# A two-layer diffusion trunk whose instruction order is planned with other durations

## The chip, the cores and the metric

The kernel runs on one NeuronCore of a Trainium2 chip. The metric is the device time of one execution in microseconds (us). Three runs of the kernel before gave 1421.18, 1422.88 and 1425.69 us; the median is 1422.88 us.

## The reference, cut to what matters

The reference is a trunk of two layers over 256 latent tokens and 256 context tokens, each of width 1024. Each layer does this:

```
mod          = silu(c) @ w_ada + b_ada                      # shifts, scales and gates, 6 x 1024
a            = rms_norm(h) * (1 + scale) + shift
p            = a @ w_in                                     # one input projection for three mixers
fa           = real 2-D Fourier transform of p's first 512 columns
db           = differential attention, 4 heads, two softmaxes each, with rotary embedding
nc           = neighbourhood attention, 8 heads, with a position bias
y            = (sig(g_a)*(fa@w_a) + sig(g_b)*(db@w_b) + sig(g_c)*(nc@w_c)) @ w_out
h            = h + gate * y
f            = rms_norm(h) * (1 + scale2) + shift2
h            = h + gate2 * (silu(conv(f@w_up_a)) * conv(f@w_up_b)) @ w_down     # 2 x 2816 wide
```

Layer 0 computes latent and context tokens (512 tokens), layer 1 only the latent ones for all that comes after keys and values (256 tokens). The result is the final RMS norm of the latent stream. Everything is float32.

## The kernel before

**Products.** Each float32 product is made of three passes over rounded values: every operand is split into a high part (rounded to the format that TensorE reads quickly, `F32R`) and a low part (the rest). `three()` (L246, matmuls on L250) and `tok_part()` (L267, matmuls on L276) multiply high by high, high by low and low by high into one PSUM bank. A matmul of layer 0 has 512 columns, one of layer 1 has 256.

**Weights.** `unit()` (L103) brings 512 KB of weights (128 x 1024) in by one DMA from SyncE (L100) into one of four raw buffers `wr`; ScalarE (ACT) makes the high part by a cast (L110), VectorE (DVE) the low part by a subtraction (L111). There are three pairs of split buffers, `wa`, `wb` and `wc`, used in turn. One unit feeds 24 matmuls of `feat()` (8 blocks of the inner dimension, three passes each).

**Stages.** The stretches of the trace, in us from the span's start, are these:

- 0 to 36: inputs, first modulation vectors, first norms; 36 to 107: values and keys in token layout (`tok_part`).
- 107 to 285: attention of layer 0. There are eight items, four heads of differential attention (`diff_head`, L351) and four pairs of neighbourhood heads (`na_pair`, L401), in turn. `project()` (L624) makes queries and keys of the next item by two `feat_tile`s and is written ahead of the item itself.
- 285 to 462: the three branch projections, gates and merge (L681 to L707).
- 462 to 570: output projection, residual, second norm. 570 to 853: the feed-forward (conv, silu, `w_down`).
- 853 to 960: layer 1's norm and token-layout products. 960 to 1138: attention of layer 1 with the Fourier mixer at its end. Layer 1 also computes the pre-activations of one of the gates there (L646, L647) and keeps them in `h`.
- 1138 to 1245: merge, output projection and norm of layer 1. 1245 to 1406: feed-forward. 1406 to the end: final norm and output.

**Attention on the engines.** A tile of scores is made in one of three PSUM banks `sc` (two matmuls, L337 and L339). In `na_pair` DVE adds the bias (L432) and takes the maximum (L434), ACT takes the exponential (L437), DVE scales (L408, L409), TensorE transposes (L414), ACT copies the transpose to SBUF (L415), TensorE multiplies by the values (L421). The bank of the scores is free again after the exponential. In `diff_head` the same steps are L364, L366, L369 to L372, L306, L308 and L377. The accumulators of the projections are two banks `pp`; a `pp` bank is free when queries or keys have been copied out (`rope`, `stack_k`, `stack_q`, L317 to L349).

**Sigmoids.** The merge takes the sigmoid of a gate into a tile `p` of a pool with three buffers. In layer 1 that pool is open during the attention. The sigmoid of the one gate whose pre-activations lie in `h` is L694, the others are on L697 (straight from the accumulator).

**What sets the order.** The Python code writes all instructions once, in one sequence. The framework's scheduler then plays the program through in a model of time, and in it hands each engine, whenever that engine is free, the earliest written of those of its instructions whose inputs and buffers are ready. The result is one fixed list for each engine (TensorE, VectorE, ScalarE, GpSimd, and SyncE for the DMAs), and on the chip every engine works its list strictly in order, waiting where an input isn't there. So the durations in the model decide which matmul of the next item stands between which two steps of this one. In the lists of before, long stretches of TensorE's keep the written order (merge and feed-forward of both layers); the matmuls of L250 in the attention stages are cut into short groups, with scores, transposes and value products of the item before in between.

## Time and profile before

| | |
|---|---|
| median of three runs | 1422.88 us |
| the profiled execution | 1424.49 us |
| its span, first to last instruction | 1422.7 us |
| TensorE busy | 1378.5 us, 97% |
| VectorE busy | 938.0 us, 66% |
| ScalarE busy | 686.7 us, 48% |
| GpSimd busy | 144.0 us, 10% |
| mean granted TensorE clock | 0.99 |
| DMA | 206 MB, 145 GB/s over the span |

The busy time of an engine is the union of its instructions' records; what is missing to the span is time in which the engine ran nothing. The granted clock is the share of TensorE's full 2.4 GHz that was granted; 0.5 is its lower level, 1.2 GHz. "L250 PE MATMUL pp<-aH,wch" is a matmul of line 250 with output tile `pp` and the inputs `aH` and `wch`. `PE` is TensorE, `PEld` its weight loads, `DVE` VectorE, `ACT` ScalarE, `POOL` GpSimd. "A <- B" in a list of waits says that A's engine had nothing to do until B ended.

### The profile page before, as it was taken

The page shows a single profiled execution, that of the slowest core. Times are in us where ns is not written, and L with a number is a line of the kernel's source. Part 1 is how long each engine was busy: PE and PEld are TensorE (multiplying, and loading weights), DVE is VectorE, ACT ScalarE, POOL GpSimd, SP SyncE. Part 2 cuts the span into 40 slices and gives each one's busy share as a digit, 9 for nine tenths or more (in the row PEclk, how much of TensorE's full clock was granted, in tenths as well). Part 3 has the DMA queues.
Part 4 walks back from the last instruction along what each step waited for, and adds up shares of the span by engine and source line. Part 5 has one row for each costly group of instructions (what it writes and reads, how often), then busy time and mean ns, then how long its engine had stood idle before and what let it go on. Part 6 is the DMA issues. An engine that isn't in the chain of part 4 may idle for free. (4 is left out here: it accounts for less than half of the span.)

```text
span 1422.7 us, 21634 instructions
## 1 busy us (share of the span) xinstructions
PE 1378.5 (97%) x8470; PEld 1206.7 (85%) x8470; DVE 938.0 (66%) x1552; ACT 686.7 (48%) x1188; POOL 144.0 (10%) x136
## 2 busy tenths in 40 slices
PE   6999999999999999999999999999998999999998
PEld 4887778888888798888888888998787899899997
DVE  3447876487877747878877573527677456788843
ACT  4547776532222335443433222527666545666643
POOL 1100000011211230000000021201000012200001
PEclk9999999999999999999999999999999999999999
DMA  7732211256556322444645682423333355466663
GB/s 274 260 107 75 74 57 48 75 165 219 180 190 197 129 75 89 149 148 134 206 136 168 200 264 91 152 89 111 97 90 104 95 188 177 146 190 187 185 177 97
DMA packets 60390, 206.14 MB, mean 145 GB/s; under 512 B 6656, under 2 KB 9088, under 8 KB 60288
## 3 DMA queue, kind: packets, MB, share of 16 engines
q1 hardware_dynamic: 60288, 204.76, 45.4%
q8 instruction: 66, 1.08, 0.3%
q14 instruction: 36, 0.29, 0.1%
HBM read 203.69 MB, written 1.05 MB: 144 GB/s over the span
## 5 line engine op out<-in xcount | busy, mean ns | idle before, releaser
L111 DVE TENSOR_TENSOR wcl<-wr,wch 128x1024 fp32r<-128x1024 f32 x93 | 114.8, 1234 | 92.4 <-ACT wch L110 92.4
L110 ACT CAST wch<-wr 128x1024 fp32r<-128x1024 f32 x93 | 97.7, 1051 | 145.2 <-PE pp L250 51.8
L110 ACT CAST wbh<-wr 128x1024 fp32r<-128x1024 f32 (+1 forms) x93 | 96.0, 1032 | 137.0 <-PE pp L250 47.5
L110 ACT CAST wah<-wr 128x1024 fp32r<-128x1024 f32 (+1 forms) x94 | 97.0, 1032 | 129.4 <-PE pp L250 33.0
L111 DVE TENSOR_TENSOR wbl<-wr,wbh 128x1024 fp32r<-128x1024 f32 (+1 forms) x93 | 111.5, 1199 | 69.6 <-ACT wbh L110 69.6
L111 DVE TENSOR_TENSOR wal<-wr,wah 128x1024 fp32r<-128x1024 f32 (+1 forms) x94 | 112.8, 1200 | 47.7 <-ACT wah L110 47.1
L250 PE MATMUL pp<-aH,wch 128*128 128x256 f32 (+1 forms) x272 | 90.9, 334 | 1.2 <-ACT aH L231 1.2
L250 PE MATMUL pp<-aH,wcl 128*128 128x256 f32 (+1 forms) x272 | 90.7, 333 | 0.0
L250 PE MATMUL pp<-aL,wch 128*128 128x256 f32 (+1 forms) x272 | 90.3, 332 | 0.0
L158 DVE SCALAR_TENSOR_TENSOR wr<-wr,cr 128x1024 f32<-128x1024 f32 x44 | 55.4, 1258 | 40.4 <-DMA wr<-in_wadaT 40.2
L250 PE MATMUL pp<-aL,wbh 128*128 128x512 f32 (+1 forms) x216 | 77.6, 359 | 1.4 <-DVE aL L707 1.4
L250 PE MATMUL pp<-aH,wbh 128*128 128x512 f32 (+1 forms) x216 | 78.1, 362 | 0.0
L250 PE MATMUL pp<-aH,wbl 128*128 128x512 f32 (+1 forms) x216 | 77.8, 360 | 0.0
L703 POOL TENSOR_TENSOR m<-m,o 128x512 f32<-128x512 f32 (+1 forms) x32 | 46.2, 1444 | 288.4 <-DVE o L702 288.4
L187 POOL TENSOR_TENSOR sqa<-sqa,t 128x256 f32<-128x256 f32 x18 | 21.2, 1193 | 492.6 <-DMA wr<-in_wdn 264.1
L250 PE MATMUL pp<-aH,wah 128*128 128x256 f32 (+1 forms) x200 | 66.4, 332 | 1.5 <-DVE ks L332 1.5
L250 PE MATMUL pp<-aH,wal 128*128 128x256 f32 (+1 forms) x200 | 66.0, 330 | 0.0
L250 PE MATMUL pp<-aL,wah 128*128 128x256 f32 (+1 forms) x200 | 65.8, 329 | 0.0
L250 PE MATMUL sc<-aL,wah 128*128 128x512 f32 (+1 forms) x192 | 64.6, 336 | 0.4 <-DVE aL L707 0.4
L250 PE MATMUL sc<-aH,wah 128*128 128x512 f32 (+1 forms) x192 | 64.6, 336 | 0.0
L250 PE MATMUL sc<-aH,wal 128*128 128x512 f32 (+1 forms) x192 | 64.3, 335 | 0.0
L250 PE MATMUL sc<-aH,wch 128*128 128x512 f32 (+1 forms) x184 | 62.9, 342 | 0.0
(403 smaller groups left out, 4294.2 us busy)
## 6 DMA issues: line engine op xcount, KB each, us to landing
wr<-in_wup SPq DMA_DIRECT2D x88, 512.0 KB, 3.6
wr<-in_wint SPq DMA_DIRECT2D x80, 512.0 KB, 3.6
wr<-in_wadaT SPq DMA_DIRECT2D x44, 512.0 KB, 3.5
ar<-in_wadaT SPq DMA_DIRECT2D x36, 512.0 KB, 3.6
wr<-in_wdn SPq DMA_DIRECT2D x32, 512.0 KB, 3.9
wr<-in_wink SPq DMA_DIRECT2D x24, 512.0 KB, 3.6
wr<-in_wabc SPq DMA_DIRECT2D x24, 512.0 KB, 3.6
wr<-in_wada SPq DMA_DIRECT2D x16, 512.0 KB, 5.8
```

The costliest lines, as they stand in the source:

```text
L110: act.copy(hi[:, :n], t[:, :n])
L111: state["lo"].tensor_tensor(out=lo[:, :n], in0=t[:, :n], in1=hi[:, :n].bitcast(F32), op=ALU.subtract)
L158: dve.scalar_tensor_tensor(out=scr, in0=w, scalar=1.0, in1=crs[s], op0=ALU.mult, op1=ALU.mult, accum_out=mods[l][:, m, s:s + 1])
L187: eng.tensor_tensor(out=sqa[:, c], in0=sqa[:, c], in1=sq, op=ALU.add)
L250: pe.matmul(acc, lhsT=a, rhs=b, start=(first and i == 0 and z == 0), stop=(last and i == n - 1 and z == 2))
L703: pool.tensor_tensor(out=m_, in0=m_, in1=t, op=ALU.add)
```

## The change

```diff
-    with tile.TileContext(nc) as tc:
+    with tile.TileContext(nc, schedule_with_timeline_sim=True) as tc:
         trunk(tc, *args)
```

This is all of it. The instructions, their operands and the written sequence stay as they are. The scheduler takes the durations by which it plays the program through from another model, a simulation of the program's timeline on all devices, instead of its simple one. Each engine's list, and with it the waits between the engines and the turn in which buffers are handed out, comes from that.

## Rows read from the trace of the kernel before

**Rows 1.** The page's first part: span, busy time and share of each engine.
```profile
span 1422.7 us, 21634 instructions
PE 1378.5 (97%) x8470; PEld 1206.7 (85%) x8470; DVE 938.0 (66%) x1552; ACT 686.7 (48%) x1188; POOL 144.0 (10%) x136
```
**Rows 2.** Busy time by stage: stretch, its length, busy us of each engine (instructions), clock, DMA.
```profile
0.00:36.00 36.00, 21.92 (x155) 16.47 (x156) 13.42 (x36) 14.84 (x31) 5.64 (x10) 0.91 0.78 273
107.00:285.00 178.00, 176.47 (x1074) 143.32 (x1073) 122.28 (x290) 118.15 (x284) 10.38 (x10) 1.00 0.21 66
285.00:462.00 177.00, 177.00 (x783) 146.61 (x781) 140.69 (x193) 49.55 (x57) 29.58 (x14) 1.00 0.60 191
462.00:570.00 108.00, 103.26 (x593) 89.84 (x592) 70.04 (x107) 48.84 (x82) 25.26 (x25) 1.00 0.32 98
570.00:853.00 283.00, 283.00 (x1250) 234.35 (x1249) 207.29 (x294) 106.39 (x139) 10.71 (x8) 1.00 0.55 175
960.00:1138.00 178.00, 165.92 (x1068) 141.91 (x1067) 119.52 (x238) 117.21 (x229) 11.87 (x16) 0.97 0.33 99
1209.00:1245.00 36.00, 32.85 (x258) 32.11 (x258) 25.08 (x44) 22.45 (x39) 8.88 (x9) 0.91 0.47 146
1245.00:1406.00 161.00, 160.94 (x1364) 159.84 (x1363) 120.37 (x181) 93.30 (x147) 5.63 (x5) 1.00 0.59 178
```
**Rows 3.** TensorE's waits, 960 to 1138 us: us in total, times, longest us.
```profile
PE sc L337 <- ACT p L437: 6.2, 4, 2.1
PE sc L474 <- ACT p L437: 1.5, 1, 1.5
PE pp L250 <- DVE ks L332: 1.5, 1, 1.5
PE sc L337 <- ACT p L366: 1.2, 3, 0.6
PE tr L414 <- DVE p L409: 1.0, 1, 1.0
PE tr L414 <- ACT qs L320: 0.6, 1, 0.6
```
**Rows 4.** TensorE's timeline at two waits: start, duration, instruction, [idle before, releaser].
```profile
998.72 0.50 PE L337 MATMUL sc<-ks,qs 128*128 128x512 f32 x1 [1.84 <-ACT p L437]
...
1067.28 0.39 PE L250 MATMUL pp<-aL,wbh 128*128 128x512 f32 x1
1069.75 0.77 PE L337 MATMUL sc<-ks,qs 128*128 128x512 f32 x1 [2.08 <-ACT p L437]
1070.74 0.63 PE L250 MATMUL pp<-aH,wbl 128*128 128x512 f32 x1
```
**Rows 5.** ScalarE's timeline around 995 us and at 1102 us, in layer 1's attention.
```profile
994.87 1.28 ACT L694 ACT_TABLE_LOAD   x1
996.16 0.42 ACT L694 ACTIVATE p<-h 128x256 f32<-128x256 f32 x1
996.60 1.28 ACT L437 ACT_TABLE_LOAD   x1
...
1102.59 1.28 ACT L437 ACT_TABLE_LOAD   x1
```
**Rows 6.** The granted clock (third number from the end) in two short stretches of that stage.
```profile
1067.00:1077.00 10.00, 7.92 (x37) 6.19 (x35) 7.97 (x20) 6.47 (x17) 0.00 (x0) 0.83 0.49 157
1104.00:1111.00 7.00, 6.29 (x20) 4.86 (x20) 2.50 (x8) 4.38 (x11) 0.00 (x0) 0.52 0.05 19
```
**Rows 7.** The casts of L110 and the loads of weights: duration; size and time to landing.
```profile
L110 ACT CAST wch<-wr 128x1024 fp32r<-128x1024 f32 x93 | 97.7, 1051 | 145.2 <-PE pp L250 51.8
L111 DVE TENSOR_TENSOR wcl<-wr,wch 128x1024 fp32r<-128x1024 f32 x93 | 114.8, 1234 | 92.4 <-ACT wch L110 92.4
wr<-in_wint SPq DMA_DIRECT2D x80, 512.0 KB, 3.6
```

## The prediction

> **What bounds the kernel now.** I read the page's busy shares first, then busy time by stage, then TensorE's waits in the stage with the most idle time, then the timelines at its longest waits. TensorE is busy for 1378.5 of 1422.7 us, the next engine, VectorE, for 938.0 [rows 1]. The change removes no matmul, so a better order can give back only TensorE's idle time, 1422.7 − 1378.5 = 44.2 us, and time lost at the lower clock. By stage [rows 2] the idle time is very uneven: 0.0 in the merge (285 to 462), 0.0 and 0.1 in the two feed-forwards (570 to 853, 1245 to 1406), 1.5 in the attention of layer 0 (178.0 − 176.47), 12.1 in the attention of layer 1 (178.0 − 165.92), 4.7 around the second norm of layer 0, 3.2 around that of layer 1, 14.1 in the first 36 us. The reader is to see that more than 620 us of the span have nothing to gain, and that two stages of equal length and nearly equal work differ eightfold.
>
> In layer 1's attention the waits name the reason [rows 3]: of the six groups, four that sum to 10.1 us end with an exponential of ACT or the scaling on DVE behind it (6.2 + 1.5 + 1.2 + 1.0). TensorE's next matmul needs a score bank, or the scores' successor, that the list promised sooner than ACT and DVE deliver it. In layer 0 the same promise holds, because a filling matmul there has 512 columns and covers twice the time.
>
> **The change part by part.** The sum is made against the profiled execution, 1424.49 us (span 1422.7 us and 1.8 us around it); the median of the runs is 1.6 us lower, and I carry the difference over to it. The change adds, removes and resizes nothing; it moves instructions in five lists, so each term below is a wait that goes or comes.
>
> *Layer 1's attention, waits with ready work behind them.* At 1069.75 us TensorE has sat 2.08 us for a score bank, and 1.0 us later takes up the projection matmul that it could have run meanwhile; that one waits for nothing [rows 4]. A list made with durations closer to the chip's would put the scores later. The clock goes with it: in the 10 us from 1067 it averages 0.83 [rows 6], a loss of 10 × (1 − 0.83) = 1.7 us that follows this stall, at the lower of the two levels, 1.2 GHz. Together 3.8 us. The remaining waits of these kinds, which no row shows to have ready work behind them, are 6.2 − 2.08 − 1.84 = 2.3 for L337, 1.2, 1.0 and 0.6 [rows 3, 4], together 5.1 us; I take half, 2.5. Work moved ahead as a filler is missing later in the same stage: I charge 1.0 us for that, half of one such stall. Net 3.8 + 2.5 − 1.0 = 5.3 us gained. The bounds: all of 12.1 idle, the 1.7, and 7.0 × (1 − 0.52) = 3.4 at the lower clock from 1104 [rows 6] is 17.2 gained; the loss has its bound in the last rival.
>
> *Layer 1's attention, sigmoids among the exponentials.* ACT runs one sigmoid of the merge early, at 996.16, between two table loads of 1.28 us; the exponential behind the second releases TensorE after 1.84 us of idle time [rows 4, 5]. At 1102.59 another load stands in front of an exponential, and the Fourier mixer's first matmul waits 1.5 us for it [rows 3, 5]. Their price on TensorE is 1.84 + 1.5 = 3.3 us and, at most, the 3.4 us at the lower clock that follows. The sigmoid is ready as soon as its input is, and under any durations ACT has idle moments there (117 of 178 us busy [rows 2]), so I take no change here: 0, with 6.7 us gained as one end. The pool of `p` has three buffers, so not more than three sigmoids can stand that early; the other end is one more pair of loads that TensorE waits out, 2 × 1.28 = 2.6 us lost.
>
> The Trainium skill, page "ScalarE: Activation LUTs", section "Rules for kernel authors", says to group transcendentals by table set, and budgets about 2.7 us for a switch. The measured load here is 1.28 us, so the measurement decides on the size; on the mechanism the trace agrees. By the page's figure an early sigmoid with its two switches would be 5.4 us of ACT, an estimate from that page, and grouping would be worth about twice the above.
>
> *The transitions.* At the start and around the norms each engine waits for one other in a chain (square, sum, power, broadcast, scale, cast). Where nothing else is ready, no order helps: 0. The bounds are half of the idle time in 462 to 570 and 1209 to 1245 either way, (4.7 + 3.2) / 2 = 4, and for the first 36 us as much as the clock there takes already, 36 × (1 − 0.91) = 3.2, either way.
>
> *Layer 0's attention.* 1.5 us can go at most; I take 0, and price the loss as a rival.
>
> *Merge and feed-forward.* TensorE has no idle time there and long runs in written order: 0 gained. What hides the other engines is a supply of split weights: four raw buffers and three split pairs. VectorE is busy for 207 of 283 and 120 of 161 us [rows 2], so it recovers. If a list put one unit late by the whole chain, the price would be one load, one cast and one subtraction, 3.6 + 1.05 + 1.23 = 5.9 us [rows 7], less the units in stock; I take 0.
>
> *The queues.* SyncE's list is also new. A load that moves ahead of another in it waits there for its buffer and holds up all loads behind it; a load behind a transfer of its own size in the same queue is late by no more than one landing, 3.6 us [rows 7], which the four buffers cover in full stages. GpSimd is busy for 144 us [rows 1]; its steps stand in chains already counted.
>
> The sum: 1424.49 − 5.3 = 1419.2 us for a profiled execution; from the median, 1422.88 − 5.3 = 1417.6 us, 0.37% less.
>
> **The rivals.**
>
> *The waits only move.* TensorE in layer 1's attention is busy 93% of the time, ACT and DVE two thirds each, and every tile of scores runs through both in turn. If that chain with three score banks is the limit, a stall removed at one bank comes back at the next. For it: L337 alone waits seven times [rows 3], not at one place. Against it: layer 0's 1.5 us with the same three banks. The time would be the old one, within 0.3%, 4.3 us, which is about what a measurement of this kernel can tell from no change: 1419 to 1427. Here also belongs that the other durations hardly change the lists, for which the long stretches in written order speak: 1422.9.
>
> *The sigmoids leave the exponentials.* If the new durations leave ACT no gap at 995 and 1101 us, the loads there go, with 6.7 us. With the 5.3 that makes 1422.88 − 12.0 = 1410.9. For it: the gaps are short. Against it: nothing but a gap is needed.
>
> *Layer 0's attention gets what layer 1's has* (slower). A model in which a step of ACT or DVE, or the wait between two engines, looks shorter than on the chip puts scores and transposes earlier; TensorE then stands at each of them. This order is now good by 10.6 us against the other layer's (12.1 − 1.5), and there too the clock fell: 1.7 + 3.4. The price is up to 10.6 + 5.1 = 15.7 us, if layer 1 stays as it is: 1438.6. It decides from the point where layer 0's idle time grows by more than layer 1's falls by 4.3, that is from 5.3 + 4.3 = 9.6 us with the forecast's gain, or 4.3 without it. For it: in layer 0 there is hardly anything to gain and any other cut of the fills can only cost. Against it: a simulation of all devices should place them better than a simple model.
>
> The Trainium skill, page "TensorE: Matmul & The Clock Gate", section "A second HAM failure mode: psum-queue depth-cycling", reports that micro-idles between groups of matmuls are enough to make the clock swing. The rows here bear that out only for long ones: layer 1's attention, cut into short groups throughout, was granted 0.97. By that rule this rival would cost more: an estimate from it, half of a 178 us stage at the lower level, would be 45 us, and I give it 2 in 100 within the rival.
>
> **How the numbers follow.** The forecast has a chance of 0.34, the sigmoids' leaving 0.08, waits that only move 0.28, the slower rival 0.30. So faster by over 0.3% is 0.42, within 0.3% 0.28, slower 0.30. The likeliest case's own range is 1411 to 1418.6 us (the half taken of the waits without shown ready work can be all or nothing, and the transitions can give 4). The whole range goes from 1406, where forecast, sigmoids and transitions come together (1422.88 − 5.3 − 6.7 − 4 = 1406.9), to 1439, where the slower rival pays its price in full. Outside I leave 0.05 below and 0.10 above, the latter for the slower rival together with a longer start.
>
> **What would show it.** Right: TensorE's idle time between 960 and 1138 us falls from 12.1 to 5 or 7 us; the wait of L337 for L437 falls from 6.2 to below 3; the clock doesn't drop around 1070; idle time in the full stages stays at 0. The table loads at 995 and 1101 stay. Wrong: idle time above 4 us in 107 to 285, more than three early sigmoids' loads, TensorE waiting for weights in a feed-forward, or an unchanged sum of waits at other lines.

## The result, and the profile after

The kernel after takes 1436.06 us (median of 4 runs, 1435.42 to 1436.91), before on the same chip 1422.03 us (4 runs, 1419.74 to 1425.69): a ratio of 1.0097, 95% interval 1.0074 to 1.0119. The forecast was 1417.6 us and faster. The time lies in the range given, on the other side of the forecast. A ratio and its interval are formed from runs that aren't over 1.5% above the fastest of the same kernel, which leaves out one run in all that follows, 2755.24 us of u_att0.

The page of the profiled execution after (1436.91 us), first part, answers to [rows 1]:

```profile
span 1435.1 us, 21653 instructions
PE 1375.2 (96%) x8470; PEld 1209.4 (84%) x8470; DVE 933.5 (65%) x1552; ACT 681.9 (48%) x1188; POOL 137.2 (10%) x136
```

The matmuls are the same 8470. TensorE is busy 3.3 us less and idle 59.9 us in place of 44.2. To see where, I cut each trace at the same instructions on TensorE: the first score product of a layer (L337), the statistics of a norm (first L199) and its last broadcast (L216). The lengths in us, and in brackets TensorE's idle time, summed from its instructions' records:

```
                              before       after       difference
start, to layer 0's scores    103.1 (14.1) 108.9 (19.4)   +5.8
attention and merge, layer 0  409.0 ( 3.2) 415.9 ( 9.5)   +6.9
second norm                    22.1 ( 1.4)  21.7 ( 2.0)   -0.4
feed-forward, layer 0         347.4 ( 1.9) 354.8 ( 6.0)   +7.4
norm and tokens, layer 1       87.6 ( 0.9)  91.0 ( 3.3)   +3.4
attention and merge, layer 1  248.9 (12.6) 241.5 ( 9.7)   -7.4
second norm                     3.9 ( 1.9)   3.8 ( 1.8)   -0.1
feed-forward, layer 1         192.3 ( 1.2) 189.1 ( 1.2)   -3.2
final norm                      8.4 ( 7.1)   8.4 ( 7.1)    0.0
span                         1422.7       1435.1         +12.4
```

Layer 1 got more than was forecast, 10.7 us, but by the brackets only 3.0 us of it are idle time (15.7 before, 12.7 after, over its last three stages ahead of the final norm); the rest came out of TensorE's busy time. Layer 0, the start and layer 1's token products lost 23.5 (5.8 + 6.9 + 7.4 + 3.4).

TensorE's waits after, in four stretches: the start (0 to 40 us), layer 0's attention (110 to 292), its feed-forward (560 to 875), and layer 1's attention (968 to 1150), which answers to [rows 3]. Columns: what waited and for whom, us in total, times, longest.

```profile
PE o L199 <- DVE p L187: 15.1, 2, 9.5
...
PE sc L337 <- ACT p L437: 5.0, 3, 3.5
...
PE tr L250 <- DVE wal L111: 1.6, 1, 1.6
PE sc L250 <- DVE wal L111: 1.4, 2, 0.9
PE pp L250 <- DVE wal L111: 1.1, 1, 1.1
...
PE sc L337 <- ACT p L437: 4.9, 1, 4.9
PE sc L337 <- ACT p L366: 2.9, 3, 1.6
```

The reader is to see three new kinds: a second wait for statistics in the start, a wait for scores in layer 0, and waits for split weights in a feed-forward that had none. In layer 1 the four waits of 6.2 us for L437 have become one of 4.9, and the three for L366 grew from 1.2 [rows 3] to 2.9.

By windows, the stages of after that answer to [rows 2] (start, layer 0's attention, layer 1's attention) and the stretch behind the wait of 3.5 us; the third number from the end is the granted clock:

```profile
0.00:42.00 42.00, 24.68 (x184) 19.17 (x188) 13.72 (x39) 16.28 (x33) 5.83 (x10) 1.00 0.83 300
112.00:290.00 178.00, 170.62 (x1021) 142.14 (x1020) 120.84 (x282) 113.15 (x270) 8.78 (x10) 0.98 0.21 63
...
967.00:1146.00 179.00, 170.27 (x1109) 147.71 (x1108) 115.69 (x232) 116.18 (x228) 9.60 (x13) 0.97 0.32 97
...
143.00:150.00 7.00, 5.66 (x24) 5.14 (x24) 6.84 (x24) 5.65 (x17) 0.00 (x0) 0.52 0.20 71
```

Layer 0's attention has 7.4 us idle where before had 1.5, and 7 us at the lower level (1.2 GHz), a loss of up to 7.0 x (1 - 0.52) = 3.4 us.

### The profile page after: what moved, and what is told of

Same layout as the page of the kernel before. It is cut to its first block, busy times and chain, and to the rows that moved or that the text cites. A ratio compares the mean times of both kernels' runs of the same rounds, so it can differ in the third digit from the quotient of the medians.

```text
span 1435.1 us, 21653 instructions
## 1 busy us (share of the span) xinstructions
PE 1375.2 (96%) x8470; PEld 1209.4 (84%) x8470; DVE 933.5 (65%) x1552; ACT 681.9 (48%) x1188; POOL 137.2 (10%) x136
## 4 chain that ended last, share of the span: by engine, by line
PE 76%; DVE 7%; DMA 7%; ACT 6%; issue 3%; POOL 1%; DVEq 0%; SPq 0%; POOLq 0%; ACTq 0%
PE pp L250 27%; PE sc L250 19%; PE tr L250 12%; PE pp L276 7%; DMA wr<-in_wadaT 6%; PE o L421 2%; PE sc L276 1%; PE o L377 1%; DVE wal L111 1%; PE sc L337 1%; DVE wr L158 1%; DVE wbl L111 1%; PE sc L474 1%; PE sc L339 1%; DVE wcl L111 1%
## 5 line engine op out<-in xcount | busy, mean ns | idle before, releaser
L111 DVE TENSOR_TENSOR wcl<-wr,wch 128x1024 fp32r<-128x1024 f32 x93 | 114.2, 1228 | 87.9 <-ACT wch L110 87.1
L110 ACT CAST wah<-wr 128x1024 fp32r<-128x1024 f32 (+1 forms) x94 | 96.9, 1031 | 150.4 <-PE sc L250 48.9
L110 ACT CAST wbh<-wr 128x1024 fp32r<-128x1024 f32 (+1 forms) x93 | 96.0, 1032 | 143.4 <-PE pp L250 51.8
L110 ACT CAST wch<-wr 128x1024 fp32r<-128x1024 f32 x93 | 97.6, 1050 | 137.7 <-PE pp L250 50.3
L111 DVE TENSOR_TENSOR wal<-wr,wah 128x1024 fp32r<-128x1024 f32 (+1 forms) x94 | 113.3, 1205 | 66.7 <-ACT wah L110 65.9
L111 DVE TENSOR_TENSOR wbl<-wr,wbh 128x1024 fp32r<-128x1024 f32 (+1 forms) x93 | 112.7, 1212 | 65.8 <-ACT wbh L110 64.9
L250 PE MATMUL pp<-aH,wch 128*128 128x256 f32 (+1 forms) x272 | 90.3, 332 | 1.2 <-ACT aH L231 1.2
L250 PE MATMUL pp<-aL,wch 128*128 128x256 f32 (+1 forms) x272 | 90.0, 331 | 0.0
L250 PE MATMUL pp<-aH,wcl 128*128 128x256 f32 (+1 forms) x272 | 89.9, 330 | 0.0
L158 DVE SCALAR_TENSOR_TENSOR wr<-wr,cr 128x1024 f32<-128x1024 f32 x44 | 53.8, 1223 | 54.3 <-DMA wr<-in_wadaT 54.0
L250 PE MATMUL pp<-aH,wbh 128*128 128x512 f32 (+1 forms) x216 | 77.7, 360 | 0.4 <-DVE ql L325 0.4
L250 PE MATMUL pp<-aL,wbh 128*128 128x512 f32 (+1 forms) x216 | 77.2, 357 | 0.0
L250 PE MATMUL pp<-aH,wbl 128*128 128x512 f32 (+1 forms) x216 | 77.0, 356 | 0.0
L250 PE MATMUL pp<-aH,wah 128*128 128x256 f32 (+1 forms) x200 | 66.2, 331 | 0.1
L187 POOL TENSOR_TENSOR sqa<-sqa,t 128x256 f32<-128x256 f32 x18 | 18.3, 1029 | 500.6 <-DMA wr<-in_wdn 266.8
L250 PE MATMUL pp<-aL,wah 128*128 128x256 f32 (+1 forms) x200 | 66.1, 331 | 0.0
L250 PE MATMUL pp<-aH,wal 128*128 128x256 f32 (+1 forms) x200 | 65.9, 330 | 0.0
L250 PE MATMUL sc<-aH,wah 128*128 128x512 f32 (+1 forms) x192 | 64.6, 336 | 0.9 <-ACT wah L110 0.9
L250 PE MATMUL sc<-aH,wal 128*128 128x512 f32 (+1 forms) x192 | 64.5, 336 | 0.5 <-DVE wal L111 0.5
L250 PE MATMUL sc<-aL,wah 128*128 128x512 f32 (+1 forms) x192 | 64.5, 336 | 0.0
L250 PE MATMUL sc<-aH,wcl 128*128 128x512 f32 (+1 forms) x184 | 63.1, 343 | 0.0
```

The source lines that it names most:

```text
L110: act.copy(hi[:, :n], t[:, :n])
L111: state["lo"].tensor_tensor(out=lo[:, :n], in0=t[:, :n], in1=hi[:, :n].bitcast(F32), op=ALU.subtract)
L158: dve.scalar_tensor_tensor(out=scr, in0=w, scalar=1.0, in1=crs[s], op0=ALU.mult, op1=ALU.mult, accum_out=mods[l][:, m, s:s + 1])
L187: eng.tensor_tensor(out=sqa[:, c], in0=sqa[:, c], in1=sq, op=ALU.add)
L250: pe.matmul(acc, lhsT=a, rhs=b, start=(first and i == 0 and z == 0), stop=(last and i == n - 1 and z == 2))
```

## The experiments

All runs are compared with before on the same chip, 3 or 5 rounds. The ratio is not the quotient of the two medians, and where the runs of a kernel spread the two differ: in u_start 1431.12 / 1422.90 is 1.0058, the ratio 1.0033. Where two changed kernels are compared by their medians, these can be of different chips; the stage lengths of the traces stand beside them. Nothing is computed otherwise in any of them: each adds only edges of issue order, so that an engine's instructions go in a list written out in the kernel. The helper is this; `LISTS` stands for the lists named in each diff:

```diff
+def _pin(tc, orders):
+    info = mybir.DependencyInfo(mybir.DependencyClass.NoSync, mybir.DependencyReason.DATA)
+    for order in orders:
+        for a, b in zip(order, order[1:]):
+            tc.add_manual_dep(known[b], a, info, reason="pin")
...
         trunk(tc, *args)
+        _pin(tc, LISTS)
```

What isn't pinned stays with the scheduler of the base kernel, and came out as there, except in how neighbouring groups of instructions alternate at a border.

### Which stages lose

Theory 1: each stage has its own price. Theory 2: one early delay pushes the rest. Theory 3: what is saved in one place is waited out in another.

```diff
+        LISTS = before's, all five engines, start              # u_start
+        LISTS = before's, all five engines, layer 0's attention  # u_att0
+        LISTS = before's, all five engines, layer 0's feed-forward  # u_ffn0
+        LISTS = the three together                             # u_three
```

> The changed kernel, but on all five engines the instructions written up to the first stage's end (inputs, first norms, values and keys in token layout) stand in the order of the kernel before. Theory 1 (each stage's new order loses its own time): the first stage took 108.9 us to the first score matmul against 103.1 before, so 5.7 us come back: 1430.4 us, ratio to the kernel before 1.0057. Theory 2 (one early delay shifts everything that follows out of step with the plan, and the later waits are its consequence): more comes back than that, 1436 - 12 to 1436 - 20, that is 1416 to 1424 us. Theory 3 (what is saved here is waited out at the next stage): 1435 to 1437.

Measured: 1431.12 us, ratio 1.0033 (1.0015 to 1.0050); the start 105.6 us.

> The changed kernel with the order of before, on all engines, in the attention of layer 0 only. Theory 1: that stage, from the first score matmul to the output projection's norm, took 415.9 us against 409.0, so 6.9 us come back: 1429.2 us, ratio 1.0048. Theory 2: the waits in this stage come from the late start, not from its own order: less than 3 us comes back, 1433 to 1436. Theory 3: 1435 to 1437.

Measured: 1432.03 us, 1.0042 (1.0022 to 1.0063); attention and merge 412.5 us, without time at the lower clock. The profiled execution is the fastest of the ten, 1427.09 us; its start, where TensorE's list came out otherwise at the border to the attention, took 106.1 us.

> The changed kernel with the order of before in the feed-forward of layer 0 only. TensorE, GpSimd and SyncE have the same order there in both kernels, so this exchanges VectorE's and ScalarE's lists of one stage. Theory 1: the stage took 355.4 us against 347.7, so 7.7 us come back: 1428.4 us, ratio 1.0042, and TensorE no longer waits for the split wal on L111. Theory 2 (late start): the waits stay, 1434 to 1436. Rival of its own (the loads themselves are late and VectorE's list doesn't matter): the waits for wal stay, 1435 to 1437.

Measured: 1431.12 us, 1.0047 (1.0031 to 1.0063); the feed-forward 350.1 us.

> The changed kernel with the order of before in all three of these stages; transitions, merges and the whole of layer 1 keep the new order. Theory 1: 1436.1 - 5.7 - 6.9 - 7.7 = 1415.8 us, ratio 0.995, faster than the kernel before, because layer 1 keeps what the new order gains there (5.6 us by the milestones of the two traces). Theory 2 gives the same sum or less, 1416 to 1424. Theory 3: above 1425.

Measured: 1422.69 us, 0.9988 (0.9972 to 1.0004). That is 7 us above Theory 1's figure and inside Theory 2's range, so it is the single edits and the stage lengths that decide. By medians the single edits give 4.9, 4.0 and 4.9 us against after's 1436.06, 13.9 in sum, and the three together 13.4. By the ratios they give 9, 8 and 7 us, 24 in sum, and the three together 15.5; so the times alone don't settle whether the edits add up. The traces do: with before's lists the start takes 105.6 us alone and 105.4 here, attention and merge 412.5 and 411.6, the feed-forward 350.1 and 349.9, while with after's lists it stays at 108.4 to 110.9, 415.8 to 416.1 and 354.0 to 357.8 (nine traces each). In u_start the two later stages stay at 416.1 and 354.4 though the start is early. That is Theory 1; Theories 2 and 3 fall. With the three undone the kernel should have been faster than before by layer 1's gain, and wasn't: each of the three stays 2 to 4 us longer than in before (103.1, 409.0, 347.4), which is Theory 1's miss, and layer 1's norm and token products still take 90.6 us in place of 87.6. The next run undoes these too:

```diff
+        LISTS = u_three's and before's, layer 1's norm and token products
```

> The kernel after, with the order of before in four stretches: the start, layer 0's attention, layer 0's feed-forward, and layer 1's norm and token products; after's order stays in layer 0's merge and from layer 1's attention on. The pinned three stretches alone gave 0.9988. Theory 1: the fourth gives back 4 to 5 us more (69.3 us of token products back to 64.5), ratio 0.995 to 0.996, and equal within 0.2% to the kernel that has after's order in layer 1 alone. Rival: the 4.8 us of the token products are no matter of their order (a pace or a clock that follows from what went before): 0.998 to 0.999, token products still near 69 us.

Measured: 1418.23 us, 0.9964 (0.9949 to 0.9978); norm and tokens 87.2 us in place of 90.6. A fourth stage with a price of its own: 3.4 us by the traces and by the ratios, 4.5 by the medians. In after TensorE waits there for split weights too, 1.6 us and less.

### Is layer 1's gain real

```diff
-        # base: the kernel after
+        # base: the kernel before
+        LISTS = before's up to layer 1's tokens; after's in layer 1's attention; after's from its merge on
```

> All lists in the order of before up to layer 1's token products, in the order of after from layer 1's attention on. Theory 1 (each stage has its own price, and layer 1 did gain): attention and merge of layer 1 take 241 us instead of 249, its feed-forward 189 instead of 192, and the whole is 9 to 11 us under before: ratio 0.993 (0.991 to 0.995). Theory 3 (the profiled executions differ by chance there, and the gain isn't in the order, or is waited out): ratio 0.998 to 1.001, attention and merge 246 us or more.

Measured: 1406.48 us (5 runs, 1406.31 to 1407.24), ratio 0.9880 (0.9857 to 0.9902): the fastest of all, below the lowest ratio expected, 0.991. The edit wasn't what its expectation says. Attention and merge were pinned as two groups, and how they alternate was left to the simple model; it came out as in neither kernel. The clean form pins both as one:

```diff
-        LISTS = ...; after's in layer 1's attention; after's from its merge on
+        LISTS = ...; after's from layer 1's attention on, as one list for each engine
```

> All lists in the order of before up to layer 1's token products; from there on exactly after's lists, also in how attention and the work of the merge alternate (the earlier kernel of this kind had left that alternation to the simple model, and came out at 1406.5 us, ratio 0.988, with 234 us for attention and merge of layer 1 in place of 249). Theory 1 (layer 1 gains what the two traces show, 7.4 us in attention and merge and 3.2 in the feed-forward): 241 to 242 and 189 us, ratio 0.993 (0.991 to 0.9945), with the wait of 4.9 us for an exponential behind a sigmoid's two table loads still there. Rival (what ran before decides over layer 1's waits): 234 to 237 us, the wait of 4.9 us gone, ratio 0.988 to 0.990.

Measured: 1413.86 us (6 runs, 1413.67 to 1415.31), 0.9939 (0.9921 to 0.9956); attention and merge 240.1 us, feed-forward 188.8. Theory 1: after's order is worth 9.3 us in layer 1 by the medians of 6 and 11 runs. One pair of traces doesn't size its attention, as before's own lists took 248.9 us there in before's trace and 243.3 in z_bsp's. The loss elsewhere is 1436.06 - 1413.86 = 22.2 us. Of the gap between this kernel and w_four, 4.4 us, the traces put 1.4 us in the start, 2.1 in attention and merge of layer 0 and 1.4 in its feed-forward, where w_four leaves the merge and the borders of the pinned groups to after's lists; no run separates these.

Of the 7.4 us between the two kernels the traces put 5.7 in attention and merge of layer 1 (240.1 and 234.4 us). ScalarE's timeline after at that place shows one reason:

```profile
1115.23 1.04 ACT L110 CAST wbh<-wr 128x1024 fp32r<-128x1024 f32 x1
1116.29 1.28 ACT L697 ACT_TABLE_LOAD   x1
1117.59 0.47 ACT L697 ACTIVATE p<-pp,sm 128x256 f32<-128x256 f32 x1
1118.08 1.28 ACT L437 ACT_TABLE_LOAD   x1
1119.37 0.69 ACT L437 ACTIVATE p<-sc,st 128x512 f32<-128x512 f32 x1
```

A sigmoid of the merge stands between two table loads ahead of the exponential that holds the score bank: the wait of 4.89 us from 1115.31. In the kernel at 1406.5 us the same sigmoid comes at 1097.26, behind the four exponentials, with one load. Two edits move it:

```diff
         # base: the kernel after, all lists pinned
+        ScalarE: the early sigmoid (L697) behind the four exponentials (L437)     # y_sig
...
         # base: y_l1
+        ScalarE: the same
+        TensorE: eight value products (L377) ahead of the 24 matmuls of a merge product  # z_end1
```

> The kernel after with one instruction moved on ScalarE: the early sigmoid of the merge (L697), which stands between two table loads ahead of the last four exponentials of layer 1's attention, goes behind them. Theory (the sigmoid and its loads are on TensorE's path): the wait of 4.89 us falls by 1.28 + 0.47 + 1.28 = 3.0 to about 1.9, and up to 3.4 us at the lower clock behind it go too: 3 to 6 us less than after, ratio 1.0045 to 1.0075. Rival (the bank held longer by the sigmoid, or the value products listed late, set the end): the wait moves to another matmul, ratio 1.008 to 1.010.

Measured: 1433.50 us, 1.0077 (1.0059 to 1.0095), so 2.6 us; attention and merge 238.0 us in place of 241.5. That is just under the theory's range, and the interval holds the rival's 1.008 too: the wait of 4.9 fell to 1.7, and part of it moved, as the Fourier mixer's (L474) grew from 0.4 to 1.7:

```profile
PE sc L337 <- ACT p L437: 1.7, 1, 1.7
PE sc L474 <- ACT p L437: 1.7, 1, 1.7
```

> Before's order up to layer 1's token products and after's from there on (1413.9 us, attention and merge of layer 1 240.1), with two moves at the end of that attention: the early sigmoid goes behind the four exponentials, and eight value products (L377) go ahead of the 24 matmuls of a merge product that stood among them. Theory (the two together are what the kernel at 1406.5 us has better): 234 to 236 us for the stage, no wait above 1.2 us for L437 on L337, ratio 0.988 to 0.990. Rival (the rest of the alternation of attention and merge matters): 237 to 240 us, ratio 0.991 to 0.994.

Measured: 1408.24 us, 0.9898 (0.9880 to 0.9915), 5.6 us less than y_l1; the stage 236.6 us, 3.5 less. The ratio is as the theory has it, the stage 0.6 us above its range, and a wait of 1.7 us for L437 is left. So the sigmoid and the value products are most of it, 3.5 of 5.7 us by the traces, not all; what each is worth alone on this base wasn't run. TensorE's waits there (950 to 1150 us) in z_end1; y_l1 has after's two, 4.9 and 2.9 us:

```profile
PE sc L337 <- ACT p L366: 2.9, 3, 1.6
PE sc L337 <- ACT p L437: 1.7, 1, 1.7
PE sc L474 <- ACT p L437: 1.3, 1, 1.3
```

### The start

After's TensorE takes the statistics of the second half of the tokens ahead of all token products, and waits 5.61 us for them.

```diff
+        LISTS = before's, ScalarE alone, start                       # w_startact
+        LISTS = before's, TensorE, ScalarE, VectorE, GpSimd, start   # z_startpad
...
         # base: the kernel before, all lists pinned
+        LISTS = after's, SyncE alone, start                          # z_bsp
```

> The kernel after with ScalarE's list alone in the order of before in the start (up to 108.9 us); TensorE keeps the statistics of the second norm ahead of all token products. Theory T (TensorE's order is the price: it stands 5.6 us at the statistics with ready products behind them): that wait stays at 5 us or more, the stage within 1.5 us of 108.9, ratio 1.008 to 1.011. Rival A (ScalarE's casts and two early silu set the statistics' time): the wait falls below 3 us, the stage to 106 us or less, ratio 1.005 to 1.008.

Measured: 1449.69 us, 1.0186 (1.0165 to 1.0207); the start 121.0 us. Both theories missed. The wait for statistics didn't stay, it grew to 14.4 us. One engine's list of before among four of after is out of step with them; which of its steps is, isn't shown.

> The kernel after with the lists of TensorE, ScalarE, VectorE and GpSimd in the order of before in the start; SyncE's list of loads stays after's. ScalarE's alone made the start 12 us longer, all five 3.3 us shorter than after's 108.9. Theory C (the order of the compute engines together makes the start's loss): 104 to 106.5 us, ratio 1.005 to 1.007. Rival Q (the order of the loads on SyncE makes it): 108 us or more, ratio 1.009 or more.

Measured: 1439.79 us, 1.0119 (1.0099 to 1.0139); the start 110.6 us. Rival Q: with the compute engines' order of before, and after's loads, nothing comes back; TensorE's first wait for token products is 9.1 us.

> The kernel before with one list changed: SyncE's in the start is after's, in which seven loads that are needed later (the second half of the tokens, a constant, two of the repeated conditioning vector, two position biases) go ahead of the three weight loads for the first token products. With after's loads and the compute engines in the order of before the start had taken 110.6 us, with all five lists of before 105.6. Theory Q (the order of the loads alone makes the start's loss): TensorE's first wait for token products (2.4 us) becomes 6 us or more, the start goes from 103 to 107 to 111 us, ratio 1.003 to 1.006. Rival (the loads only matter together with the other engines' order or with the boundary to the attention): 105 us or less, ratio 0.998 to 1.002.

Measured: 1427.62 us against 1421.92, 1.0040 (1.0022 to 1.0058); the start 110.1 us, 7.0 more than before. (Of the seven loads named, the two position biases stayed where before has them.) Theory Q: SyncE's list alone carries it. Its queue in after and in z_bsp: start, time over which the group is issued, load, count.

```profile
3.21 1.87 SPq L100 DMA_DIRECT2D wr<-in_wada  x4
5.17 1.84 SPq L535 DMA_DIRECT2D h<-in_xT  x2
7.06 3.10 SPq L582 DMA_DIRECT2D cst<-in_const  x1
10.20 0.91 SPq L595 DMA_DIRECT2D cr<-in_crep  x2
11.15 1.33 SPq L428 DMA_DIRECT2D nab<-in_nab  x2
13.54 3.28 SPq L100 DMA_DIRECT2D wr<-in_wink  x3
```

```profile
5.14 1.81 SPq L535 DMA_DIRECT2D h<-in_xT  x2
6.99 2.96 SPq L582 DMA_DIRECT2D cst<-in_const  x1
9.99 0.91 SPq L595 DMA_DIRECT2D cr<-in_crep  x2
11.97 2.04 SPq L100 DMA_DIRECT2D wr<-in_wink  x3
```

The three weight units of the first token products (`in_wink`) are issued in z_bsp when they are in before, but behind loads that are for later. Before, from its queue, its issues and TensorE's timeline:

```profile
11.90 2.03 SPq L100 DMA_DIRECT2D wr<-in_wink  x3
...
wr<-in_wink SPq DMA_DIRECT2D x3, 512.0 KB, 4.1
...
18.86 0.58 PE L276 MATMUL pp<-wah,aH 128*128 128x256 f32 x1 [2.65 <-ACT aH L231]
```

DMA in the first 34 us, after and then z_bsp: GB/s in 40 slices, and the issues with KB each and median us to landing.

```profile
GB/s 0 0 57 196 364 377 368 336 371 399 400 424 419 388 387 351 354 402 405 414 408 405 383 395 419 407 400 419 414 328 87 10 125 308 313 371 318 357 82 48
...
wr<-in_wink SPq DMA_DIRECT2D x3, 512.0 KB, 9.6
cr<-in_crep SPq DMA_DIRECT2D x2, 512.0 KB, 9.6
cst<-in_const SPq DMA_DIRECT2D x1, 671.5 KB, 11.0
```

```profile
wr<-in_wink SPq DMA_DIRECT2D x3, 512.0 KB, 10.2
```

And TensorE's wait there in z_bsp:

```profile
PE pp L276 <- ACT aH L231: 8.8, 1, 8.8
```

They land 9.6 and 10.2 us after issue, before 4.1. The activations that TensorE's wait is put down to (L231) stand in ScalarE's list behind the casts of these units: the first cast starts at 15.56 us in before, and in z_bsp at 21.78, after 6.66 us of waiting for the DMA. So TensorE waits 8.8 us ahead of the token products in z_bsp, in before 2.65. The five loads are 2 x 512 + 671.5 + 2 x 512 = 2720 KB (of 1024 bytes); at some 400 GB/s, as in the slices from 8 to 24 us, that is an estimate of 7.0 us, and the start grew by 7.0 in the trace, the whole by 5.7.

### Layer 0's feed-forward

TensorE, GpSimd and SyncE have the same lists here in both kernels, but for TensorE's first matmuls at the border to the second norm; ScalarE and VectorE don't. Three edits on after:

```diff
+        LISTS = before's, VectorE alone, layer 0's feed-forward                         # w_ffndve
+        LISTS = before's, ScalarE alone, layer 0's feed-forward                         # w_ffnact
+        LISTS = before's, VectorE alone, its second half, the products with w_down     # z_down
```

> The kernel after with VectorE's list alone in the order of before in layer 0's feed-forward; ScalarE's list of that stage stays after's, and TensorE's, GpSimd's and SyncE's are the same in both kernels there. Theory D (VectorE stands at modulation pieces whose weights are still on their way, with the weight split behind them): the waits of L250 for the split on L111 go, the stage takes 350 us instead of 355, ratio 1.005 to 1.006. Rival S (ScalarE's casts come late): the stage stays at 354 or more, ratio 1.009 to 1.010.

Measured: 1439.30 us, 1.0111 (1.0090 to 1.0132); the stage 359.4 us. Both missed: not better, 4.6 us worse than after, and above all traces with after's lists (354.0 to 357.8).

> The kernel after with ScalarE's list alone in the order of before in layer 0's feed-forward; VectorE's list stays after's. With VectorE's alone the stage took 359.4 us (after 354.8), with both lists 350.1. Theory P (ScalarE's and VectorE's lists have to fit each other, either alone is out of step): 354 us or more, ratio 1.009 to 1.012. Rival S (ScalarE's order is the cause): 350 to 351 us, ratio 1.005 to 1.007.

Measured: 1446.50 us, 1.0164 (1.0144 to 1.0185); the stage 365.6 us. Theory P in its sign, with a price beyond its range: 14.8 us of idle time. In the first half after takes each cast and the split behind it some steps earlier, on both engines; to undo it on one would set them against each other, which is read from the lists and not tested by itself.

> The kernel after with VectorE's list in the order of before in the second half of layer 0's feed-forward alone, the products with w_down, where the lists of the other four engines are equal in both kernels. There after's list has the modulation pieces (L158), which wait for DMAs, one to three steps further up, ahead of weight splits. Theory M (these pieces are what TensorE waits for through the splits): its waits for L111 between 830 and 870 us (0.87, 1.62, 1.10) go, the stage takes 350 to 351 us, ratio 1.0055 to 1.007. Rival (the first half, where after takes casts and splits one unit earlier, costs the time): 354 us or more, ratio 1.009 to 1.010.

Measured: 1429.55 us, 1.0045 (1.0029 to 1.0061), the stage 349.0 us, a little better than expected. In the second half only VectorE's list differs. After has the modulation pieces (L158) further up; each works in place on weights that a DMA brings. VectorE's timeline after, around TensorE's wait of 1.62 us from 850.71:

```profile
847.30 1.23 DVE L158 SCALAR_TENSOR_TENSOR wr<-wr,cr 128x1024 f32<-128x1024 f32 x1 [2.40 <-DMA wr<-in_wadaT]
848.45 0.08 DVE L158 DVE_READ_ACCUMULATOR wr<-wr,cr 128x1 f32 x1
849.90 1.23 DVE L158 SCALAR_TENSOR_TENSOR wr<-wr,cr 128x1024 f32<-128x1024 f32 x1 [1.36 <-DMA wr<-in_wadaT]
851.05 0.08 DVE L158 DVE_READ_ACCUMULATOR wr<-wr,cr 128x1 f32 x1
851.05 1.22 DVE L111 TENSOR_TENSOR wal<-wr,wah 128x1024 fp32r<-128x1024 f32 x1
```

VectorE stands 2.40 and 1.36 us for pieces that nobody needs yet, and the split that TensorE needs is behind them. VectorE's waits from 570 to 875 us in after, and in z_down:

```profile
DVE wr L158 <- DMA wr<-in_wadaT: 54.0, 29, 4.6
```

```profile
DVE wr L158 <- DMA wr<-in_wadaT: 43.7, 26, 4.6
```

TensorE's waits for L111 in the products with w_down, 3.6 us in after, are gone in z_down, and that half takes 112.6 us in before and in z_down, 117.6 in after. The other half takes 234.8 us in before and 237.1 in after; there, from 546 to 553 us, at the border to the second norm, after's clock is at 0.51.

### Layer 0's attention

TensorE after at its longest wait there (start, duration, instruction, idle before and releaser):

```profile
138.41 0.60 PE L377 MATMUL o<-v,wT 128*128 128x128 f32 x4
142.50 0.50 PE L337 MATMUL sc<-ks,qs 128*128 128x512 f32 x1 [3.48 <-ACT p L437]
...
144.57 0.58 PE L337 MATMUL sc<-ks,qs 128*128 128x256 f32 x1 [1.34 <-ACT p L437]
```

The value product at 138.41 stands behind 17 projection matmuls, the squares of its result and the maxima behind a weight split. Three edits on after tried to repair the place:

```diff
         # x_head
+        TensorE: last value product of the head 14 matmuls up
+        ScalarE: its squares and two exponentials ahead of the next cast (L110)
+        VectorE: its steps and two maxima ahead of the next split (L111)
...
         # z_head
+        the same, and: a third maximum and exponential and the scalings (L409) ahead
...
         # z_fill
+        TensorE: the value product up; 13 projection matmuls behind the fourth and the sixth score tile
+        ScalarE, VectorE: the cast and the split behind the fourth exponential
```

> The kernel after with 14 instructions moved at one place of layer 0's attention (128 to 145 us), the end of the first differential head: its last value product goes 14 matmuls up in TensorE's list, and the steps behind it go ahead of the next weight split on ScalarE and VectorE. Theory A (this one misplaced end makes the two stalls of 3.48 and 1.34 us, and the lower clock behind them): both fall below 1.2 us, no lower clock there, layer 0's attention and merge take 409 to 412 us instead of 416: ratio 1.0045 to 1.007 against before. Rival B (the stage loses at many places, a stall taken away comes back at the next score tile): the stage stays at 414 us or more, ratio 1.008 to 1.010.

Measured: 1436.82 us, 1.0090 (1.0069 to 1.0110); the stage 415.4 us. Rival B: the wait of 3.48 went, one of 2.78 for a scaling behind the same split came.

> The earlier edit at the end of the first differential head (value product up, its squares, maxima and exponentials ahead of the next weight split) changed the wait of 3.48 us into one of 2.78 for a scaling that still stood behind the split on VectorE. Here the scalings and a third maximum and exponential go ahead of the split too. Theory A (this place is worth its waits and the clock): no wait above 1.2 us is left between 136 and 152 us, layer 0's attention and merge take 409 to 412 us in place of 415.9, ratio 1.005 to 1.007. Rival B (the stall turns up once more at another line): the stage stays at 414 or more, ratio 1.008 to 1.010.

Measured: 1436.23 us, 1.0096 (1.0078 to 1.0114); the stage 415.0 us. Rival B again: 3.1 us for the fourth exponential.

> Two edits at the stall of layer 0's attention moved the waits (4.8 us) to other lines and left the stage at 415 us. After's TensorE has no projection matmul between 138.6 and 155.2 us there; the ones that could fill were run in a block just before. Here 13 of that block (L250) go down, six behind the fourth score tile of the neighbourhood heads and seven behind the sixth, with the value product ahead of them as before, and the weight split and its cast go behind the fourth exponential. Theory F (the fill is missing, not the order of the steps): 13 x 0.23 = 3.0 us of the waits are covered, the lower clock behind them goes, the stage takes 409 to 412.5 us, ratio 1.0045 to 1.0075. Rival (the time of the stage is set further along, by queries and keys that now come 3 us later): 414.5 us or more with a new wait of L337 for L320, L331 or L323, ratio 1.008 to 1.011.

Measured: 1438.28 us, 1.0084 (1.0058 to 1.0109); the stage 418.7 us. These are the rival's numbers, but not by the wait that it names: the fill was taken from ahead of the wait, which came 2 us earlier (2.97 us at 136.75), and the matmuls that were to fill ran at the lower clock. The profiled execution is the slowest of the six. Whether the fill was the lack isn't settled by this.

TensorE's waits for these three, 112 to 160 us (the last to 200), in that order:

```profile
PE tr L414 <- DVE p L409: 2.8, 1, 2.8
```

```profile
PE sc L337 <- ACT p L437: 4.5, 2, 3.1
```

```profile
PE sc L337 <- ACT p L437: 3.0, 1, 3.0
PE sc L337 <- ACT p L452: 1.6, 3, 1.1
```

Before's lists for the whole stage take the wait away (u_att0), no edit of mine at the one place did. What in those lists does it stays open. Of the 3.5 us by which u_att0's stage is still longer than before's, 2.1 are two waits at the beginning of the merge (L482 for L477, 1.2; L250 for a cast, 0.9), which before hasn't.

## Why the prediction was wrong

*What bounds the kernel.* The step that failed: every stage but layer 1's attention was put at 0, the full ones because a better order "can give back only TensorE's idle time" and time lost at the lower clock. From that follows what a full stage can gain, not what it can lose, and five lists were made anew there too. The sum had one gain and no loss; the runs show 23.5 us of losses in four stages that stood at 0 or in no term. The premise isn't right as it stands either. Layer 1 gave back 10.7 us with 3.0 us less idle time, and its feed-forward 3.2 us with none to give (1.2 us in both): the order changed TensorE's busy time, by the pace at which matmuls follow each other, and no run tells why.

*Layer 1's attention.* Forecast 5.3 us; y_l1 shows 9.3 for layer 1, of which the traces of before and after put 7.4 in this stage. The stall before L250 at 1067 is gone, as predicted, and idle time fell by 2.9 us, from 12.6 to 9.7; in the windows of [rows 2] and of after it is 8.7 in place of 12.1, not 5 or 7. The clock is as before, 0.97 [rows 2]. So the gain came for the smaller part by the step forecast, and that it isn't smaller than forecast is luck. One of its sums is off: the four groups of waits make 9.9 us, not 10.1, which changes nothing behind it. The forecast had no gain in the feed-forward (3.2).

*Sigmoids.* Put at 0 with +2.6 and -6.7 as ends. After has the early sigmoids still, and the one near the end now costs a wait of 4.9 us where it cost 1.5 [rows 3]. Taking it off the path, with eight value products moved up, was worth 5.6 us in z_end1, 3.5 of it in this stage's trace; the 6.7 priced for that rival was for sigmoids alone. The Trainium skill, page "ScalarE: Activation LUTs", section "Rules for kernel authors", says to group transcendentals by table set. By that rule the sigmoid belongs behind the exponentials; y_sig agrees, with 2.6 us for one sigmoid and its loads of 1.28 us each.

*The start and the queues.* Put at 0 with 3.2 us as a bound and "no more than one landing" for a load behind another. Measured 5.8 in after and, from SyncE's list alone, 7.0 in the start of z_bsp and 5.7 in its whole time. The cover named for it, four buffers in full stages, isn't there in the start, and not one load went ahead but five, in a queue that was already moving 400 GB/s. The price here was that of the bytes ahead at that rate.

*Feed-forward.* "VectorE recovers" failed. The price named for a late unit, 5.9 us, was taken at 0. That it is near the 7.4 measured is chance: idle time grew by 4.1 us, in several waits for splits of 1.6 us and less, not one late unit. VectorE's spare time (207 of 283 us busy [rows 2]) is no cover when an instruction in its list waits for a DMA: what stands behind it is late however idle the engine is. The prediction asked only whether TensorE's own loads were late, not what else waits in VectorE's list.

*Layer 0's attention.* The slower rival came in kind: TensorE stands at score tiles whose banks aren't free yet, and the clock falls with it, at 6.9 us and not 15.7, and below the 9.6 us from which it decides. That a step looks shorter in the model than on the chip, its reason, no run shows. It alone would have left the time within 0.3% of before. What made the kernel slower is four places at once; losses in more than one stage were named only for a time above the range, as this rival with a longer start. So that the time lies within the range is luck: its upper end is the full price of one stage, and what came is four smaller losses less a gain twice the forecast's. The Trainium skill, page "TensorE: Matmul & The Clock Gate", section "A second HAM failure mode: psum-queue depth-cycling", would have had the clock swing through the stage; the trace doesn't bear that out, 0.98 over 178 us, one drop behind one long wait.

*Token products of layer 1* had no term at all: 3.4 us in after's trace, and 3.4 in w_four's put back.

## What to carry to other kernels

When a change makes all lists anew, price the full stages too: they have no idle time to give back, and an instruction that waits for a DMA, placed ahead of a step on TensorE's path, is one way in which they lose. Judge such lists together: one engine's list of a stage put back where other engines' differ too was worse than either kernel (1.011, 1.016 and 1.019 against 1.0097), while whole stages put back together kept the lengths that each had alone. And choose by stage: after's order in layer 1 with before's elsewhere is 0.6% faster than before, 1.0% with a sigmoid moved out from among the exponentials and eight value products moved up, and 1.2% in a form that differs from it in more than these.

## What the runs showed of the hardware

The runs of before spread from 1418 to 1432 us over all chips, those of w_l1 on one from 1406.3 to 1407.2. Layer 1's attention is part of it: before's lists there took 248.9 us in before's trace and 243.3 in z_bsp's, with the same idle time, 12.6 us. The clock differs, 0.97 in [rows 2], and in z_bsp from 967 to 1145 us 0.99:

```profile
967.00:1145.00 178.00, 166.05 (x1099) 142.97 (x1099) 121.72 (x239) 118.05 (x230) 11.89 (x16) 0.99 0.34 103
```

So the same waits drop the clock in one execution and not in another. Layer 1's feed-forward takes 192.3 us with before's lists (before, z_bsp) and 188.6 to 189.5 in the eighteen traces with after's, with 1.2 to 1.4 us idle in both; from one matmul of L250 to the next it is 120.4 ns on average in before and 118.4 in after. So the difference is in how closely the 256-column matmuls follow each other, and no run tells why.
